# The last b projections of a gated convolution by seven products instead of eight, with their weight sums prepared during attention

## The chip, the cores and the metric

The kernel runs on one core of one Trainium2 chip. The metric is the device time of one execution in microseconds, as the median of several runs. TensorE, the matrix engine, is PE in the profile, and its weight loads are PEld. VectorE is DVE, ScalarE is ACT, GpSimd is POOL, and SyncE, which here only issues transfers, is SP.

## The reference

512 tokens of width 1024 pass through two layers. The first layer's mixer is attention with a forget gate and 16 heads, the second layer's is a short gated convolution; each is followed by an MLP of width 4096 and a gated embedding. What the change touches:

```python
def short_conv(h, w_in, conv_w, w_out):
    proj = h @ w_in
    b_gate, c_gate, u = proj[..., :D], proj[..., D:2 * D], proj[..., 2 * D:]
    z = c_gate * u
    zc = causal depthwise convolution of z with three taps
    return (b_gate * zc) @ w_out
```

All of it is float32.

## The kernel before

Every float32 operand of a matmul is held as two float32r halves, hi and lo, and each product is three matmuls, hi·hi, hi·lo and lo·hi (`mm3`). Each weight tile of 128x512 is loaded by SP into one of 14 `raw` buffers (L148), cast by ACT into its hi half (L299), and subtracted by DVE into its lo half (L300). All other tiles in SBUF come from 70 pages of 128x512 that are used in turn, and results of matmuls go to the eight banks of PSUM.

The 1024 channels of the convolution are eight blocks of 128, called 0 to 7, and they are made in pairs (0,1), (2,3), (4,5) and (6,7). The names of a pair's tiles carry its first channel block. For a pair there are three projections, c, u and b. c and u are made together as a 2 by 2 block product by the Strassen-Winograd scheme: seven products (`PARTS`, 1 to 7) in place of eight, each of 24 matmuls of 256 columns (two output blocks, four blocks of depth, three matmuls each), or 168 matmuls for a pair. It needs sums of tokens, s1 to s4, which DVE makes once (`token_sums`), and sums of weights, t1 to t4, which are made in DRAM. DVE puts each product together with the others as soon as it is there (`COMBINE`, L913), out of the bank into pages. `end` then multiplies c by u (L925), `finish` convolves (ACT L836, DVE L839 twice), multiplies by b (L843) and splits the result into yh and yl (ACT L299, DVE L300). b itself is made directly, by `times_b`: for a pair 2 channel blocks x 8 blocks of depth x 3 matmuls, 48 of 512 columns.

`CONV_ORDER` says in which order products, b and `end` of the pairs are written. Behind it follows `mixer_out`, which multiplies the eight y by the output weights: eight blocks (t, n) of 128 tokens by 512 columns, each the sum over k = 0 to 7 of y of channel block k (24 matmuls of 512 columns), named co0_0 and so on (n and t).

A scheduler with its own model of time sets the order within each engine from the order in which the code is written; each engine then works its list off strictly in that order.

The weight sums are made by DRAM-to-DRAM transfers that POOL issues (`sum_weights`): for each of t1 to t4 and each of the four pairs a copy of 512 KB (L211), and later an accumulating transfer of 512 KB on top of it (L213), 32 in all. They are called one at a time, behind POOL's work in the output of attention, in the MLP of the first layer and in its embedding.

In attention, SP loads for every head the bias rows, four broadcast loads (`bias`, L596) of 64 to 256 KB into pr, prr and prl. POOL masks each (L597). DVE adds the scores to it (L616), ACT exponentiates it, POOL scales it (L622), and PE transposes it (L629).

Of the kernel before, what the change touches and what calls it, by code (L numbers as in the profile page):

```python
# [15 lines left out]
P = 128  # L16
D = 1024
S = 512
# [6 lines left out]
NEG = -1e30  # L25
PUT_OFF = 46000
LAG = 2
AHEAD = 2
STACK = 6
PAGES = 70  # L30
# [59 lines left out]
def trunk(ctx: ExitStack, tc, g4T, x, xT, pT, g, g0T, wv, wqk, bf, wo, wcs, wcb, cw, wco, wup, wdn, wpp, wpg, out):  # L90
# [104 lines left out]
        return ready[key]  # L195

    behind, ahead = {}, {}
    sums_w = {n: dram.tile([4, P, 2 * S], F32, tag=f"ws{n}", name=f"ws{n}") for n in SUMS_W}

    sum_steps = [(name, kind, i) for name, kind in SUM_STEPS for i in range(4)]  # L200

    def sum_weights():

        if not sum_steps:
            return
        of = lambda n, i: sums_w[n][i] if n in sums_w else wcs[QUARTERS.index(n), i]
        name, kind, i = sum_steps.pop(0)
        a, b = SUMS_W[name]
        with tc.issue_after(behind["add"].ins):
            if kind == "copy":  # L210
                nc.gpsimd.dma_start(sums_w[name][i], of(a, i))  # L211
            else:
# [15 lines left out]
    for l in range(2):  # L228
        if l == 0:
            for c, (_, width) in enumerate(V_CHUNKS):  # L230
                for k in range(KT * width // 512 if width < 272 else KT):
                    plan(("v", c, k), wv[c][k])
            for i in range(KT):
                for j in range(4):
                    plan(("qk", i, j), wqk[i, j])
            plan_embed(0)
            for k in range(KT):
                for n in range(2):
                    plan(("o", n, k), wo[n, k])
        else:  # L240
            for i0, i in CONV_ORDER:
                if i == "embed":
                    plan_embed(1)
                elif i == "bL" or i == "b":
                    for j in range(4):
                        plan(("b", i0, j), wcb[i0 // 2, j])
                elif i in PARTS:
                    n = PARTS[i][1]
                    src = sums_w[n] if n in sums_w else wcs[QUARTERS.index(n)]
                    for s in range(2):  # L250
                        plan(("sq", i0, s, n), src[i0 // 2][:, s * S : (s + 1) * S])
            for n in range(2):
                for k in range(KT):
# [182 lines left out]
    def soon(t, n):  # L436

        return FEW if n else SOON

    def mixer_out(kind, lhs, xs, gB, then, opened):  # L440


        mgs, sums = {}, {}
        for t, n in BLOCKS:
            if (t, n) == (2, 0):
                prepare(where[kind, 1, KT - 1] + 1 + SOON)
            at = (t, n) in opened
            ps = opened.pop((t, n)) if at else bank(f"{kind}{n}_{t}")
            for k in range(KT - 1 if at else 0, KT):
                mm3(ps, lhs(k, t), wide(kind, n, k, soon=soon(t, n)), k == 0, k == KT - 1)  # L450
            sums[t, n] = squares(ps, f"{kind}s{n}_{t}")
            mgs[t, n] = gained(ps, gB, n, f"{kind}m{n}_{t}")
            if (t, 1 - n) in mgs:
                residual(t, *([d.pop((t, i)) for i in range(2)] for d in (mgs, sums)), xs[t],
                         f"{kind}r")
                if kind == "o":
                    sum_weights()
                then(t)
                if kind == "o":
                    sum_weights()  # L460

    def embed(l, soon):

# [11 lines left out]
    def attention(hT, first_xT, g0_col, first_x, by_hand):  # L475
# [108 lines left out]
        def bias(h):  # L584


            i, e = h // 2, h % 2
            if e == 0:
                both[i] = page(f"pr{i}")
            long, rest = page(f"prl{h}"), page(f"prr{h}")  # L590
            probs[h] = [
                rest[:, 384:512], both[i][:, 256 * e : 256 * e + 256], rest[:, :384], long[:, :S],
            ]
            for b, pr in enumerate(probs[h]):
                n = (b + 1) * P
                nc.sync.dma_start(pr, neg_c[b, h : h + 1, :n].partition_broadcast(P))  # L596
                nc.gpsimd.affine_select(  # L597
                    out=pr[:, b * P : n], in_=pr[:, b * P : n], compare_op=ALU.is_ge,
                    fill=NEG, base=0, pattern=[[-1, P]], channel_multiplier=1,
                )  # L600
# [215 lines left out]
        return oT[0], banks_o  # L816

    def conv(hT, plain):
        taps = consts.tile([P, KT, 3], F32, tag="taps", name="taps")
        nc.sync.dma_start(taps, cw)  # L820
        ys = []

        def times_b(i0, lo, hi):

# [6 lines left out]
                        hT.at(lambda h: h[:, k, lo:hi]), k == 0, k == KT - 1,  # L831
                    )

        def finish(i, z, y, b):
# [8 lines left out]
            nc.vector.tensor_tensor(out=a[:, :S], in0=b, in1=a[:, :S], op=ALU.mult)  # L843
            split(y.hi[:, :S], y.lo[:, :S], a[:, :S])

        half = S // 2
# [41 lines left out]
        def product(i0, i):  # L888
# [17 lines left out]
            for item in list(rest):  # L906
                out, u, v, sign = item
                if u in have and v in have:
# [6 lines left out]
                        op=ALU.add if sign > 0 else ALU.subtract,  # L915
                    )

        def end(i0):

            have = got.pop(i0)  # L920
            for e in range(2):
                i, z = i0 + e, have[f"c1{e + 1}"]
                for h, at in enumerate((L, R)):
                    m = have[f"c{h + 1}{e + 1}"]
                    nc.vector.tensor_tensor(out=z[:, at], in0=m[:, L], in1=m[:, R], op=ALU.mult)  # L925
                y = Pair(page(f"yh{i}", F32R), page(f"yl{i}", F32R))
                finish(i, z, y, banks_b.pop((i0, e)))
                ys.append(y)

        need(0, 1)  # L930
        for i0, i in CONV_ORDER:
# [315 lines left out]
def layout(x, p, norm_g, w_attn_in, b_forget, w_attn_out, w_conv_in, conv_w, w_conv_out,  # L1247
# [24 lines left out]
    got["wo"] = tiles(np.asarray(w_attn_out)[0], 1, S)  # L1272
    b, c, u = (np.asarray(w_conv_in)[0].reshape(D, 3, KT // 2, 2, P)[:, s] for s in range(3))
    got["wcb"] = tiles(b.reshape(D, D), 2, 256)
    cu = np.stack([c, u]).reshape(2, 2, 4, P, 4, 2, P)
    got["wcs"] = cu.transpose(1, 5, 4, 3, 0, 2, 6)[[0, 0, 1, 1], [0, 1, 0, 1]].reshape(4, 4, P, 2 * S)
# [26 lines left out]
```

## Time and profile before

| what | value |
|---|---|
| median of three runs | 1215.29 us (1214.1 to 1215.66) |
| the profiled execution's own time | 1215.53 us |
| its span, first to last instruction | 1213.8 us |
| PE, DVE, ACT, POOL busy | 99%, 75%, 57%, 55% |
| mean granted clock of PE | 0.999 |

The stretches of the span, in microseconds from its start: attention up to about 225, its output up to about 257, MLP and embedding of the first layer up to 644, the convolution up to 776, its output up to 821, MLP and embedding of the second layer to the end. In the page a busy PE is one whose matmuls overlap: each is shown with a duration longer than its distance from the next, so PE's pace is read from start to start, or from the count in a window.

### The profile page before, as it was taken

The numbers are of one execution on the slowest core, as the hardware profiler recorded it, in microseconds if no ns is written. First come the engines' busy times: TensorE is split into PE (matmuls) and PEld (weight loads), VectorE is DVE, ScalarE is ACT, GpSimd is POOL, SyncE is SP. The second block draws the span as 40 slices with busy tenths as digits, with TensorE's granted clock in tenths as the row PEclk, the third lists the DMA queues.
The fourth block names the chain that finished last, engine by engine and source line by source line (L and its number), as shares of the span: only waits on it lengthen the run. The fifth ranks groups of instructions, "written<-read, shape, count | busy, mean of one in ns | idle before, by whom it ended". The sixth has DMA issues, their size and how long they took to land.

```text
span 1213.8 us, 18739 instructions
## 1 busy us (share of the span) xinstructions
PE 1203.1 (99%) x6176; PEld 1028.0 (85%) x6176; DVE 910.2 (75%) x1389; ACT 697.8 (57%) x1435; POOL 662.3 (55%) x691
## 2 busy tenths in 40 slices
PE   9999999999999999999999999999999999999997
PEld 8888888898888888888889999889888888888886
DVE  5668888575698779869867888665767886679963
ACT  7567888557634654465666555235755445535652
POOL 3057677167977798876221000017769777777420
PEclk9999999999999999999999999999999999999999
DMA  9564442673565566528357445732322442244501
GB/s 308 189 183 128 134 126 65 220 245 94 123 172 140 148 164 173 151 72 264 122 153 212 144 153 172 245 129 81 119 72 88 139 132 80 67 139 130 182 19 52
DMA packets 95377, 173.91 MB, mean 143 GB/s; under 512 B 11248, under 2 KB 18464, under 8 KB 95024
## 3 DMA queue, kind: packets, MB, share of 16 engines
q1 hardware_dynamic: 90272, 155.67, 40.1%
q0 software_dynamic: 4864, 16.78, 6.5%
q8 instruction: 49, 0.80, 0.3%
q14 instruction: 48, 0.39, 0.1%
q10 hardware_dynamic: 144, 0.26, 0.1%
HBM read 164.20 MB, written 25.25 MB: 156 GB/s over the span
## 4 chain that ended last, share of the span: by engine, by line
PE 96%; ACT 2%; DVE 1%; issue 1%; DVEq 0%; POOLq 0%; POOL 0%; ACTq 0%
PE up L293 10%; PE up L292 10%; PE up L291 10%; PE dn L293 9%; PE dn L291 8%; PE dn L292 8%; PE pg L293 2%; PE pg L291 2%; PE pg L292 2%; PE sq L293 2%; PE sq L292 2%; PE sq L291 2%; PE qk L291 2%; PE qk L292 2%; PE qk L293 2%; PE sc L610 1%
## 5 line engine op out<-in xcount | busy, mean ns | idle before, releaser
L300 DVE TENSOR_TENSOR wl<-raw,wh 128x512 fp32r<-128x512 f32 (+1 forms) x400 | 375.0, 980 | 41.7 <-ACT wh L299 37.6
L299 ACT CAST wh<-raw 128x512 fp32r<-128x512 f32 (+1 forms) x400 | 218.3, 619 | 12.4 <-DMA raw<-in_wv 3.7
L292 PE MATMUL up<-hTl,wh 128*128 128x512 f32 (+1 forms) x576 | 209.9, 366 | 0.0
L293 PE MATMUL up<-hTh,wl 128*128 128x512 f32 (+1 forms) x576 | 208.9, 365 | 0.0
L291 PE MATMUL up<-hTh,wh 128*128 128x512 f32 (+1 forms) x576 | 208.7, 366 | 0.0
L300 POOL TENSOR_TENSOR wl<-T,wh 128x512 fp32r<-128x512 f32 x112 | 157.2, 1434 | 25.4 <-ACT wh L299 24.1
L970 ACT ACTIVATE r<-up 128x512 f32<-128x512 f32 (+1 forms) x72 | 39.4, 548 | 197.3 <-PE up L293 197.3
L1018 DVE TENSOR_TENSOR acc<-dn,acc 128x512 f32<-128x512 f32 x168 | 107.8, 678 | 31.1 <-PE dn L293 31.0
L292 PEld LDWEIGHTS up<-hTl,wh 128*128 128x128 f32 x576 | 108.6, 189 | 17.5
L293 PEld LDWEIGHTS up<-hTh,wl 128*128 128x128 f32 x576 | 108.7, 189 | 17.4
L291 PEld LDWEIGHTS up<-hTh,wh 128*128 128x128 f32 x576 | 108.0, 189 | 17.6
L161 POOL TENSOR_TENSOR T<-raw,raw 128x512 f32<-128x512 f32 x56 | 85.8, 1544 | 59.7 <-DMA raw<-in_wdn 28.2
L161 POOL TENSOR_TENSOR T<-raw,T 128x512 f32<-128x512 f32 x56 | 89.0, 1589 | 2.2
L321 POOL TENSOR_SCALAR cor_r_v<-cos,cos 128x1 f32<-128x1 f32 x4 | 1.2, 302 | 155.5 <-ACT junk L337 155.5
L299 ACT CAST wh<-T 128x512 fp32r<-128x512 f32 x112 | 61.5, 617 | 10.4 <-POOL T L161 10.4
L300 DVE TENSOR_TENSOR A12l<-q,A12h 128x512 fp32r<-128x512 f32 x28 | 30.1, 1074 | 42.8 <-ACT A12h L299 42.8
L300 DVE TENSOR_TENSOR A11l<-q,A11h 128x256 fp32r<-128x256 f32 x28 | 26.1, 933 | 35.9 <-ACT A11h L299 35.9
L1025 POOL TENSOR_TENSOR acc<-acc,acc 128x512 f32<-128x512 f32 x28 | 47.1, 1714 | 10.0 <-DVE acc L1018 10.0
L299 ACT CAST S1h<-s 128x512 fp32r<-128x512 f32 x28 | 17.4, 621 | 60.8 <-POOL s L985 60.8
L293 PE MATMUL pg<-wh,hTl 128*128 128x512 f32 (+1 forms) x136 | 51.8, 381 | 0.0
L291 PE MATMUL pg<-wh,hTh 128*128 128x512 f32 (+1 forms) x136 | 51.6, 379 | 0.0
L292 PE MATMUL pg<-wl,hTh 128*128 128x512 f32 (+1 forms) x136 | 51.4, 378 | 0.0
(327 smaller groups left out, 3302.2 us busy)
## 6 DMA issues: line engine op xcount, KB each, us to landing
raw<-in_wup SPq DMA_DIRECT2D x128, 256.0 KB, 2.9
raw<-in_wdn SPq DMA_DIRECT2D x128, 256.0 KB, 2.8
wst<-in_wcs POOLq DMA_DIRECT2D x24, 512.0 KB, 6.7
raw<-in_wqk SPq DMA_DIRECT2D x32, 256.0 KB, 4.8
raw<-in_wpg SPq DMA_DIRECT2D x32, 256.0 KB, 3.2
raw<-wst SPq DMA_DIRECT2D x32, 256.0 KB, 3.6
raw<-in_wcs SPq DMA_DIRECT2D x24, 256.0 KB, 4.0
g<-in_g SPq DMA_DIRECT2D x18, 256.0 KB, 5.4
```

Of the source, the lines that this page charges most:

```text
L161: nc.gpsimd.tensor_tensor(out=B[name, p], in0=B[a, p], in1=B[b, p], op=ALU.subtract)
L291: nc.tensor.matmul(ps, a.hi, b.hi, start=start, stop=False)
L292: nc.tensor.matmul(ps, a.hi, b.lo, start=False, stop=False)
L293: nc.tensor.matmul(ps, a.lo, b.hi, start=False, stop=stop)
L299: nc.scalar.copy(hi, src)
L300: eng.tensor_tensor(out=lo, in0=src, in1=hi.bitcast(F32), op=ALU.subtract)
L321: nc.gpsimd.tensor_scalar(out=v, in0=parts[0], scalar1=parts[1], scalar2=EPS, op0=ALU.add, op1=ALU.add)
L610: nc.tensor.matmul(ps[:, :nm], at[:, b * P : n], to[:, :nm], start=s == 0, stop=s == 1)
L970: nc.scalar.activation(r[:, :n], ps[:, :n], AF.Relu)
L1018: nc.vector.tensor_tensor(out=a, in0=banks[s], in1=a, op=ALU.add)
L1025: nc.gpsimd.tensor_tensor(out=a, in0=a, in1=acc[i, s][:, :S], op=ALU.add)
```

## The change

- `UNITS` adds a fifth unit, "b", beside the four pairs. Its two column halves are b of pair (4,5) and of pair (6,7): b of the last four channel blocks is now made as one block product by the same seven products, and `times_b` is left for pairs (0,1) and (2,3) alone. Its weight sums are made with the others, so there are 20 copies and 20 accumulating transfers in place of 16 and 16.
- `CONV_ORDER` writes the "b" unit behind pair 6: the first two products of each next unit stand ahead of `end` of the one before, and its last product is 2.
- `finish` now ends with the convolution; `weigh` multiplies by b and splits. For channel blocks 4 to 7 it is called in `end("b")`, once all of b is there, in two halves of 256 columns each.
- `mixer_out` for the convolution takes k in the order 0, 1, 2, 3, 4, 6, 5, 7, and writes k = 0 to 3 of the blocks (0,0) and (1,0) first.
- The 20 copies of weight sums are issued by SP during attention, two behind each `bias(h)` from head 2 on (`copy_sums`), until they run out at head 11. POOL issues the 20 accumulating transfers alone, one for each 128 tokens of attention's output and the rest in the first MLP.

```diff
+CO_ORDER = (0, 1, 2, 3, 4, 6, 5, 7)
+CO_FIRST = 4
...
-SUMS_W = {"t1": ("b11", "b12"), "t3": ("b12", "b22"), "t2": ("t1", "b22"), "t4": ("t2", "b21")}
-SUM_STEPS = (
-    ("t1", "copy"), ("t3", "copy"), ("t1", "add"), ("t3", "add"), ("t2", "copy"), ("t2", "add"),
-    ("t4", "copy"), ("t4", "add"),
-)
+SUMS_W = {"t1": ("b11", "b12"), "t3": ("b12", "b22"), "t2": ("b22", "t1"), "t4": ("b21", "t2")}
+UNITS = (0, 2, 4, 6, "b")
...
-    + [(i0, i) for i0 in (4, 6) for i in (1, 6, 7, 5, 2, 4, 3, "b", "end")]
+    + [(4, i) for i in (1, 6, 7, 5, 2, 4, 3)] + [(6, 1), (6, 6), (4, "end")]
+    + [(6, i) for i in (7, 5, 2, 4, 3)] + [("b", 1), ("b", 6), (6, "end")]
+    + [("b", i) for i in (7, 5, 3, 4, 2, "end")]
...
+    def copy_sums():
+
+        if sum_copies:
+            n, u = sum_copies.pop(0)
+            with tc.issue_after(behind["bias"].ins):
+                nc.sync.dma_start(of(n, u), of(SUMS_W[n][0], u))
 
     def sum_weights():
 
-        if not sum_steps:
-            return
...
+        if sum_steps:
+            n, u = sum_steps.pop(0)
+            with tc.issue_after(behind["add"].ins):
                 nc.gpsimd.dma_start(
-                    sums_w[name][i], of(b, i), accum_op=ALU.add, max_dma_last_dim=2048
+                    of(n, u), of(SUMS_W[n][1], u), accum_op=ALU.add, max_dma_last_dim=2048
                 )
...
+        if kind == "co":
+            for t, n in BLOCKS[:2]:
+                ps = bank(f"{kind}{n}_{t}")
+                for k in CO_ORDER[:CO_FIRST]:
+                    mm3(ps, lhs(k, t), wide(kind, n, k, soon=SOON), k == 0, False)
+                opened[t, n] = ps, CO_ORDER[:CO_FIRST]
...
                 if c == 8 * (h // 2) - SCORED - (7 if h % 2 == 0 else 4):
                     bias(h)
+                    copy_sums()
+                    copy_sums()
...
+            if i0 == "b":
+                b = got.pop(i0)
+                for e in range(2):
+                    for i1 in (4, 6):
+                        y = Pair(page(f"yh{i1 + e}", F32R), page(f"yl{i1 + e}", F32R))
+                        weigh(halfway.pop(i1 + e), y, [
+                            (at, b[f"c{h + 1}{e + 1}"][:, R if i1 == 6 else L])
+                            for h, at in enumerate((L, R))
+                        ])
+                        ys[i1 + e] = y
+                return
```

How the instructions move, at the three places that the prediction speaks of. First PE at the passage from the convolution to its output, where b7 is b of channel block 7, and co0_0 the first output block. Before:

```order
L292 MATMUL b7_9467<-hTl_90,wh337_9323 128x512
L293 MATMUL b7_9467<-hTh_89,wl337_9324 128x512
L291 MATMUL co0_0_9574<-wh338_9343,yh0_8507 128x512
L292 MATMUL co0_0_9574<-wl338_9344,yh0_8507 128x512
L293 MATMUL co0_0_9574<-wh338_9343,yl0_8508 128x512
L291 MATMUL co0_0_9574<-wh339_9361,yh1_8518 128x512
```

Now, where sq2_b is product 2 of the new unit and its last:

```order
L297 MATMUL sq2_b_9587<-hTl_90,wh343_9426 128x256
L298 MATMUL sq2_b_9587<-hTh_89,wl343_9427 128x256
L296 MATMUL co0_0_9709<-wh344_9432,yh0_8519 128x512
L297 MATMUL co0_0_9709<-wl344_9433,yh0_8519 128x512
L298 MATMUL co0_0_9709<-wh344_9432,yl0_8520 128x512
```

The 96 matmuls of 512 columns on b4 to b7 are gone from PE's list, and 168 of 256 columns, sq1_b to sq2_b, stand in one piece ahead of the output (6037 rows of matmuls and transposes before, 6109 now).

Second, the first use of the late y. On PE, in the output stage, now (co1_2 is the block of the second column half and the third 128 tokens):

```order
L296 MATMUL co1_2_9881<-wh355_9643,yh3_8819 128x512
L297 MATMUL co1_2_9881<-wl355_9644,yh3_8819 128x512
L296 MATMUL co0_0_9709<-wh348_9550,yh4_9661 128x512
L297 MATMUL co0_0_9709<-wl348_9551,yh4_9661 128x512
L296 MATMUL co0_1_9722<-wh348_9550,yh4_9661 128x512
L298 MATMUL co0_0_9709<-wh348_9550,yl4_9662 128x512
```

The scheduler put not 24 but 60 matmuls of k = 0 to 3, on all six of the first output blocks, between the last sq2_b and the first that reads yh4; yl4 is read by the 64th and yl7 by the 73rd from the first co0_0. On DVE the work between the last product and these y now stands so (cp_b holds the last combination, za4 to za7 the convolved blocks, wl the lo halves of output weights):

```order
L934 TENSOR_TENSOR cp_b_9379<-cp_b_9379,sq2_b_9587 128x512
L305 TENSOR_TENSOR wl356_9650<-raw314_9651,wh356_9649 128x512
L864 TENSOR_TENSOR za5_9181<-U_b_9418,za5_9181 128x256
L864 TENSOR_TENSOR za7_9464<-U_b_9418,za7_9464 128x256
L305 TENSOR_TENSOR wl357_9656<-raw315_9657,wh357_9655 128x512
L864 TENSOR_TENSOR za4_9175<-V_b_9493,za4_9175 128x256
L864 TENSOR_TENSOR za6_9458<-V_b_9493,za6_9458 128x256
L864 TENSOR_TENSOR za4_9175<-cp_b_9379,za4_9175 128x256
L864 TENSOR_TENSOR za6_9458<-cp_b_9379,za6_9458 128x256
L305 TENSOR_TENSOR yl4_9662<-za4_9175,yh4_9661 128x512
L305 TENSOR_TENSOR yl6_9668<-za6_9458,yh6_9667 128x512
```

with yl5 and yl7 behind them. Before, yl4 and yl5 stood ahead of pair 6's products on DVE, and only yl6 and yl7 came this late.

Third, SP in attention, at the bias loads of heads 2 and 3. Before:

```order
L596 DMA prl2_1009<-neg_c_187 128x512
L596 DMA pr1_1008<-neg_c_187 128x256
L596 DMA prr3_1092<-neg_c_187 128x128
L596 DMA prr3_1092<-neg_c_187 128x384
L596 DMA prl3_1091<-neg_c_187 128x512
L148 DMA raw50_2009<-in_wqk 128x512
```

Now:

```order
L609 DMA prl2_1009<-neg_c_187 128x512
L212 DMA wst1_85<-in_wcs 16x8192 x2
L609 DMA pr1_1008<-neg_c_187 128x256
L609 DMA prr3_1094<-neg_c_187 128x128
L609 DMA prr3_1094<-neg_c_187 128x384
L609 DMA prl3_1093<-neg_c_187 128x512
L212 DMA wst1_85<-in_wcs 16x8192 x2
L150 DMA raw50_2025<-in_wqk 128x512
```

Two copies of 512 KB stand between the loads of the even head and those of the odd one, and two more ahead of the next weight loads; so it goes for heads 2 to 11.

More of the change, by code (lines that the diff above doesn't have):

```diff
@@ L197, in trunk @@
     behind, ahead = {}, {}
-    sums_w = {n: dram.tile([4, P, 2 * S], F32, tag=f"ws{n}", name=f"ws{n}") for n in SUMS_W}
-    sum_steps = [(name, kind, i) for name, kind in SUM_STEPS for i in range(4)]
-    def sum_weights():
-        if not sum_steps:
-            return
[L206 to L212, printed above, removed]
+    sums_w = {
+        n: dram.tile([len(UNITS), P, 2 * S], F32, tag=f"ws{n}", name=f"ws{n}") for n in SUMS_W
+    }
+    of = lambda n, u: (sums_w[n] if n in sums_w else wcs[QUARTERS.index(n)])[UNITS.index(u)]
+    sum_copies = [(n, u) for n in ("t1", "t3", "t2", "t4") for u in UNITS]
+    sum_steps = list(sum_copies)
+    def copy_sums():
[3 more added lines that the diff above has]
+                nc.sync.dma_start(of(n, u), of(SUMS_W[n][0], u))
+    def sum_weights():
+        if sum_steps:
+            n, u = sum_steps.pop(0)
+            with tc.issue_after(behind["add"].ins):
                 nc.gpsimd.dma_start(
-                    sums_w[name][i], of(b, i), accum_op=ALU.add, max_dma_last_dim=2048
+                    of(n, u), of(SUMS_W[n][1], u), accum_op=ALU.add, max_dma_last_dim=2048
                 )
@@ L248, in trunk @@
                     n = PARTS[i][1]
-                    src = sums_w[n] if n in sums_w else wcs[QUARTERS.index(n)]
                     for s in range(2):
-                        plan(("sq", i0, s, n), src[i0 // 2][:, s * S : (s + 1) * S])
+                        plan(("sq", i0, s, n), of(n, i0)[:, s * S : (s + 1) * S])
             for n in range(2):
-                for k in range(KT):
+                for k in CO_ORDER:
                     plan(("co", n, k), wco[n, k])
@@ L447, in mixer_out @@
             at = (t, n) in opened
-            ps = opened.pop((t, n)) if at else bank(f"{kind}{n}_{t}")
-            for k in range(KT - 1 if at else 0, KT):
-                mm3(ps, lhs(k, t), wide(kind, n, k, soon=soon(t, n)), k == 0, k == KT - 1)
+            ps, done = opened.pop((t, n)) if at else (bank(f"{kind}{n}_{t}"), ())
+            todo = [k for k in (CO_ORDER if kind == "co" else range(KT)) if k not in done]
+            for k in todo:
+                mm3(
+                    ps, lhs(k, t), wide(kind, n, k, soon=soon(t, n)),
+                    not done and k == todo[0], k == todo[-1],
+                )
             sums[t, n] = squares(ps, f"{kind}s{n}_{t}")
@@ L595, in bias @@
                 n = (b + 1) * P
-                nc.sync.dma_start(pr, neg_c[b, h : h + 1, :n].partition_broadcast(P))
+                behind["bias"] = nc.sync.dma_start(
+                    pr, neg_c[b, h : h + 1, :n].partition_broadcast(P)
+                )
                 nc.gpsimd.affine_select(
@@ L813, in attention @@
                     bias(h)
+                    copy_sums()
+                    copy_sums()
         for _ in main:
             pass
-        return oT[0], banks_o
+        return oT[0], {at: (ps, range(KT - 1)) for at, ps in banks_o.items()}
     def conv(hT, plain):
@@ L842, in finish, with weigh @@
                 )
-            nc.vector.tensor_tensor(out=a[:, :S], in0=b, in1=a[:, :S], op=ALU.mult)
+            return a
+        def weigh(a, y, b):
+            for at, m in b:
+                nc.vector.tensor_tensor(out=a[:, at], in0=m, in1=a[:, at], op=ALU.mult)
             split(y.hi[:, :S], y.lo[:, :S], a[:, :S])
```

19 lines of the change are left out of this document (11 added, 8 removed).

## Prediction

> **What bounds the kernel now.** I read the page first, then PE's busy time by stage, then the convolution stretch by stretch. The page's head, and the head of its chain of waits:
>
> ```profile
> span 1213.8 us, 18739 instructions
> PE 1203.1 (99%) x6176; PEld 1028.0 (85%) x6176; DVE 910.2 (75%) x1389; ACT 697.8 (57%) x1435; POOL 662.3 (55%) x691
> PE 96%; ACT 2%; DVE 1%; issue 1%; DVEq 0%; POOLq 0%; POOL 0%; ACTq 0%
> ```
>
> PE bounds it nearly alone, so a matmul saved is time saved if nothing else comes to the front. PE's idle time by stage (attention; its output, MLP and embedding; convolution with output; the second MLP), each row being stretch, length, and busy time of PE, PEld, DVE, ACT, POOL, then granted clock, DMA share, GB/s:
>
> ```profile
> 60.00:220.00 160.00, 158.44 (x834) 133.42 (x833) 131.44 (x357) 126.68 (x300) 105.52 (x174) 1.00 0.44 131
> 220.00:644.00 424.00, 423.29 (x1999) 354.32 (x1998) 325.10 (x389) 239.65 (x477) 283.70 (x262) 1.00 0.56 160
> 644.00:821.00 177.00, 177.00 (x1160) 162.82 (x1159) 133.44 (x226) 84.02 (x173) 8.54 (x17) 1.00 0.54 175
> 821.00:1206.00 385.00, 385.00 (x1833) 323.77 (x1832) 279.97 (x335) 208.56 (x406) 253.90 (x213) 1.00 0.32 100
> ```
>
> Only attention leaves PE idle for longer: 160 - 158.44 = 1.56 us, and 0.71 in the stage behind it. There is 2.27 us to be won by removing waits; everything else must come from less work. The clock is full, 1.00.
>
> **The matmuls: -1.67.** The convolution's four stretches that the change rewrites are products of pair 4, b4 and b5, products of pair 6, b6 and b7; the fifth is six blocks of the output:
>
> ```profile
> 713.96:734.11 20.15, 20.15 (x169) 20.14 (x168) 16.46 (x28) 10.88 (x20) 0.00 (x0) 1.00 0.47 157
> 734.11:745.02 10.91, 10.91 (x50) 9.02 (x49) 10.87 (x20) 1.87 (x3) 0.00 (x0) 1.00 0.88 297
> 745.02:765.17 20.15, 20.15 (x169) 20.14 (x168) 14.39 (x24) 12.12 (x22) 0.00 (x0) 1.00 0.41 130
> 765.17:776.08 10.91, 10.91 (x50) 9.02 (x49) 10.09 (x18) 1.97 (x3) 0.00 (x0) 1.00 0.94 300
> 776.08:808.73 32.65, 32.65 (x146) 26.99 (x145) 11.96 (x19) 8.49 (x21) 2.09 (x6) 1.00 0.46 160
> ```
>
> 168 narrow products take 20.15 us, 119.9 ns each; 48 of b take 10.91, 227.3 ns each; 144 of the output 32.65, 226.7 ns. (The counts in the rows hold one or two that reach in from the neighbours.) Out go 2 x 10.91 = 21.82 us, in come 168 narrow ones, 20.15: a gain of 1.67 us. One product in eight is gone, but a half-width matmul costs more than half, so 12.5% becomes 7.7%.
>
> The Trainium skill ("TensorE: Matmul & The Clock Gate", Wait — 56ns, not 53.3ns?) has warm matmuls follow each other at N / 2.4 GHz + about 2.5 ns: 215.8 ns for 512 columns and 109.2 for 256. By it the gain would be, as an estimate, 96 x 215.8 - 168 x 109.2 = 2.37 us. The rows above stand 11 ns over it at both widths, and the sum goes by the rows.
>
> **Does DVE keep up?** Durations of its work and of ACT's casts in this stage (the last two figures before the bar's end are total and mean ns):
>
> ```profile
> L300 DVE TENSOR_TENSOR wl<-raw,wh 128x512 fp32r<-128x512 f32 x78 | 49.7, 683 | 11.9 <-ACT wh L299 11.9
> L843 DVE TENSOR_TENSOR za<-b,za 128x512 f32<-128x512 f32 x8 | 5.5, 692 | 0.7
> L913 DVE TENSOR_TENSOR cp<-cp,sq 128x512 f32<-128x512 f32 x6 | 4.1, 682 | 2.8 <-PE sq L293 2.8
> L925 DVE TENSOR_TENSOR cp<-cp 128x256 f32<-128x256 f32 x4 | 1.7, 416 | 0.0
> L299 ACT CAST wh<-raw 128x512 fp32r<-128x512 f32 x79 | 43.0, 619 | 8.5 <-DMA raw<-in_wco 3.0 <-DMA raw<-in_wcs 2.9 <-DVE xb L416 1.9
> ```
>
> Eight b tiles of weights become fourteen: 6 x 0.683 = 4.1 us of DVE and 6 x 0.619 = 3.7 of ACT. Seven combinations are new: 7 x 0.682 = 4.8. Four multiplications by b (0.692) become eight of half width (0.416): +0.6. DVE gains 9.5 us of work over its 16.46 + 10.87 + 14.39 + 10.09 = 51.8 in the four stretches: 61.3 us in a stretch that is now 62.12 - 1.67 = 60.45. DVE is full there, so the last y come later. ACT has 26.8 + 3.7 and stays half idle. When is the last y late? The end of the y on DVE, and PE's first transposes of the stage behind with the DVE work that they read:
>
> ```profile
> 778.32 0.69 DVE L300 TENSOR_TENSOR yl<-za,yh 128x512 fp32r<-128x512 f32 x1 [0.69 <-ACT yh L299]
> 787.77 0.69 DVE L300 TENSOR_TENSOR wl<-raw,wh 128x512 fp32r<-128x512 f32 x1 [8.76 <-ACT wh L299]
> 807.44 0.69 DVE L409 TENSOR_TENSOR n_h<-xb,g 128x512 f32<-128x512 f32 x1
> 808.73 1.03 PE L354 MATMUL n_p<-ident,n_h 128*128 128x128 f32 x8
> ```
>
> Before, yl7 ends at 779.0, and 8.76 us of idle DVE follow. With all 9.5 us on top it ends at 788.5, with none of it at 777.3; laying DVE's rows one behind the other with the durations above and waiting for each product gives about 783. PE now begins the output at 776.08 - 1.67 = 774.41; it first reads yh4 behind 60 matmuls, 774.41 + 60 x 0.2267 = 788.0, and yl7 as the 73rd matmul, at 790.7. So the output matmuls with k = 0 to 3 hide the whole tail, by 2.2 us in the worst case and some 7 us in mine; 0. If that cover were gone (24 matmuls alone, 5.4 us), PE would wait 1 to 2 us, in the worst case 6.
>
> What is late next: co0_0 ends 4 to 5 us later than before (behind 73 matmuls, not 45), and with it the chain of norms that ends in n_h. PE reads it at 808.73 + 0.4, 1 us behind its end at 808.1. The last block that this chain waits for on ACT, co1_2, ends after 121 matmuls of the stage as before after 120, so the chain moves forward with PE; the margin stays between 0 and 1 us, and I give it nothing, with 1 us as the other bound. PSUM: no product waits for a bank, since each bank is read within some 5 us and the next product is 2.9 us long, with eight banks.
>
> **The copies on SP: +0.2.** POOL in the first heads' probabilities and the transposes that read them; SP's bias loads with their landing; waits of POOL's masks and of PE (total, times, longest); the DMA queue of the sums; and attention's output, where the copies ran before:
>
> ```profile
> 84.22 0.29 POOL L597 TENSOR_SCALAR_AFFINE_SELECT prr<-prr 128x128 f32<-128x128 f32 x1
> 85.94 0.29 POOL L597 TENSOR_SCALAR_AFFINE_SELECT prl<-prl 128x128 f32<-128x128 f32 x1
> 87.44 3.10 POOL L622 TENSOR_SCALAR prl<-prl,rs 128x512 f32<-128x512 f32 x2
> ...
> 89.74 0.27 PE L629 MATMUL pT<-ident,prl 128*128 128x128 f32 x1
> ...
> 72.44 3.11 SPq L596 DMA_DIRECT2D prr<-neg_c  x2
> 75.64 0.38 SPq L596 DMA_DIRECT2D prl<-neg_c  x1
> DMA to landing us min/median/max: 6.3/7.0/8.2
> ...
> POOL prr L597 <- DMA prr<-neg_c: 39.3, 6, 27.7
> PE ps_o L651 <- ACT ph L299: 0.8, 2, 0.5
> PE ps_o L652 <- DVE pl L300: 0.4, 1, 0.4
> ...
> q0 software_dynamic: 4864, 16.78, 6.5%
> 234.00:265.00 31.00, 31.00 (x181) 27.32 (x180) 24.47 (x39) 17.05 (x43) 15.17 (x28) 1.00 0.99 354
> ```
>
> No copy on SP is in the trace, so its price is bounded. From below by the rate of the last row: 2 x 0.524 MB / 354 GB/s = 3.0 us of all engines for a pair. From above by the queue: 6.5% of 1213.8 us over 32 transfers of 512 KB is 2.5 us each, 4.9 for a pair. I take 3.5, nearer the rate, since half of the 32 are accumulating and do more. A pair stands ahead of head 3's bias loads, which land by 74.5 + 8.2 = 82.7 and 75.64 + 6.3 = 81.9; POOL asks for them at 84.22 and 85.94, 1.5 to 4 us later. Queued behind that mask on POOL are the scalings (L622) of head 0, whose first prl ends half way through the pair, at 89.0, and PE's transpose reads it at 89.74: 0.75 us to spare. So a pair delays PE here by 0 (3.5 within the spare) up to 4.9 - 1.5 - 0.75 = 2.65 us. In the new order head 3's mask of pr stands behind two scalings on POOL and no longer ahead of them, which gives it 3 us more; I take 0.2. For later heads PE reads what POOL scales many microseconds after, and the weight loads of attention run ahead by up to 14 buffers, so a few microseconds on SP's queue reach nobody.
>
> POOL loses 16 copy issues and gains 4 accumulating ones; 8 of the 16 stood in attention's output, where PE idles next to nothing, the rest in MLP and embedding, where it does not wait for POOL: 0. The loss of 8 x 0.5 MB from the full DMA of 234 to 265 frees nobody that PE waits for: 0.
>
> **Sum:** -1.67 + 0.2 = -1.5. The profiled execution took 1215.53 us for a span of 1213.8, so 1214.0; it stood 0.24 over the median of the runs, which makes 1213.8 as a median. About 0.2%, 2.4 us, is what a measurement can tell from no change.
>
> **Rivals.**
> - *The copies reach PE.* They pass through the queue on which bias and weights come, and a head's last load is not issued before loads eight places ahead have landed. If head 3's loads come a whole pair, 4.9 us, after POOL asks, POOL stands still, the first probabilities are late, and PE loses 4.9 - 0.75 = 4.15: -1.67 + 4.15 = +2.5, 1217.8. It decides from 0.75 us of delay on POOL on. For: POOL is the third engine of this stage, and masks already wait for loads, 11.6 us in five waits beside the first of 27.7. Against: 1.5 to 4 us of spare. The Trainium skill ("DMA: Bandwidth & Descriptors", Queues, rings and completion order) says that each DMA engine serves its queue rows in turn, packet by packet; by it POOL's queue let the loads of SP slip in between, and on SP's own they must stand behind, which speaks for this rival. No row here shows copies on SP. Chance 0.1.
> - *Waits disappear too.* Heads and output of attention are reordered a little, and half of the 2.27 us of PE's idle time goes: -1.67 - 1.1 = -2.8, 1212.5. For: POOL has fewer instructions where PE waits. Against: the waits that the trace names for PE are on ACT and DVE, whose lists stay. Chance 0.15.
> - *The y come too late.* If ACT's 3.7 us add to DVE's 9.5 instead of lying beside them, yl7 ends at 792.2, 1.5 us after PE asks, and the transposes behind lose their margin too: -1.67 + 1.5 + 0.2 = 0, 1215.3. Chance 0.08.
> - *The seven products don't save what they say*, since narrow matmuls run at PEld's limit (20.14 of 20.15 us) and any disturbance of weight loads shows: gain 0.5, 1214.8. Chance 0.05.
>
> **How the numbers follow.** The forecast has 0.6, with its own range of 1213.0 to 1215.0; the rest, 0.02, is a loss that I don't see. The range for 8 in 10 reaches from the bottom of the second rival, 1212.0, to above the case of a PE wait of 2.65 us in attention, 1213.8 - 0.2 + 2.65 = 1216.2: 1212.0 to 1216.4. Faster by over 0.2% means under 1212.9: most of the second rival and the edge of the forecast, 0.2. Slower by over 0.2% means over 1217.7: the first rival's worse half and what I don't see, 0.1. Within: 0.7.
>
> **What would show it.** Right: the four stretches become three of 20.15 us with PE at 119.9 ns, the output begins 1.67 us earlier, DVE busy for nearly the whole of 714 to 783, yl7 before 788; PE's idle time from 60 to 220 within 0.5 us of 1.56. Wrong: a wait of PE for pT or ps_o at 89 to 110, masks on POOL waiting for bias loads of odd heads by more than 1.5 us, a wait of co for yh or yl, or of n_p for n_h.

## The result and the profile after

The change makes the kernel slower by 0.9%: 1226.44 us as a median (1224.92 to 1227.98) against 1215.29 for the kernel before, a ratio of 1.0093 with a 95% interval of 1.0079 to 1.0107. The profiled executions stand 10.5 us apart in their spans. Here and in the experiments, the few executions that took 40% longer or more than the others of the same kernel are left out. The head of the page after, and the head of its chain of waits:

```profile
span 1224.3 us, 18924 instructions
PE 1205.6 (98%) x6248; PEld 1033.6 (84%) x6248; DVE 909.7 (74%) x1406; ACT 700.8 (57%) x1442; POOL 659.6 (54%) x679
PE 91%; DMA 5%; ACT 1%; issue 1%; DVE 1%; SPq 1%; POOL 1%; POOLq 0%; DVEq 0%
```

The chain was 96% PE and now has 5% of DMA in it: somewhere PE follows a transfer. The stretches say where. Columns as in the prediction: attention, then one of its slices and its three stretches at half clock, then the products of pairs 4 and 6, those of unit b, and six blocks of the output.

```profile
60.00:220.00 160.00, 151.15 (x771) 127.11 (x770) 120.01 (x339) 118.91 (x281) 103.97 (x167) 0.97 0.59 182
140.00:160.00 20.00, 18.06 (x93) 15.36 (x91) 13.58 (x41) 13.29 (x34) 13.39 (x22) 0.91 0.83 242
94.31:97.73 3.42, 3.42 (x11) 2.65 (x11) 3.23 (x9) 2.43 (x7) 1.47 (x4) 0.50 0.59 198
111.38:114.79 3.41, 3.41 (x12) 2.82 (x11) 0.63 (x2) 1.18 (x4) 2.41 (x3) 0.50 0.46 154
152.34:155.75 3.41, 3.41 (x12) 2.92 (x13) 0.10 (x2) 0.46 (x1) 3.41 (x4) 0.50 0.93 234
725.95:766.26 40.31, 40.31 (x337) 40.31 (x336) 34.37 (x59) 16.77 (x31) 0.00 (x0) 1.00 0.57 185
766.26:786.42 20.16, 20.16 (x170) 20.16 (x169) 18.95 (x34) 11.18 (x21) 0.00 (x0) 1.00 0.72 216
786.42:819.07 32.65, 32.65 (x146) 27.00 (x145) 16.99 (x32) 10.19 (x24) 2.16 (x4) 1.00 0.63 215
```

The convolution did what was forecast: 40.31 + 20.16 = 60.47 us from the first product of pair 4 to the output, where it was 62.12, so 1.65 us less. Attention lost much more. PE is idle for 160 - 151.15 = 8.85 us of it, 7.3 more than before, and for 10.24 us it runs at half the clock, which costs 5.1 more. Together 7.3 + 5.1 - 1.65 = 10.8, against 10.5 in the spans.

What PE waits for in attention, the list of waits of the kernel after (total, times, longest):

```profile
PE ps_o L666 <- POOL ph L651: 5.4, 3, 3.0
PE pT L644 <- POOL prl L637: 2.7, 1, 2.7
```

The timeline of POOL and PE at the first two of them; "[2.68 <-POOL prl L637]" is the idle time ahead of an instruction and what ended it:

```profile
89.94 0.29 POOL L612 TENSOR_SCALAR_AFFINE_SELECT prl<-prl 128x128 f32<-128x128 f32 x1 [2.00 <-DMA prl<-neg_c]
90.22 1.24 POOL L637 TENSOR_SCALAR prr<-prr,rs 128x384 f32<-128x384 f32 x1
91.44 3.10 POOL L637 TENSOR_SCALAR prl<-prl,rs 128x512 f32<-128x512 f32 x2
93.06 0.33 PE L644 MATMUL pT<-ident,prl 128*128 128x128 f32 x1 [2.68 <-POOL prl L637]
109.54 0.29 POOL L612 TENSOR_SCALAR_AFFINE_SELECT prl<-prl 128x128 f32<-128x128 f32 x1 [0.87 <-DMA prl<-neg_c]
109.77 0.21 POOL L651 MEMSET ph<- 128x128 f32 x1
110.03 0.39 PE L666 MATMUL ps_o<-ph,v 128*128 128x256 f32 x1 [3.00 <-POOL ph L651]
```

It is the chain that the first rival describes. POOL stands at the mask of head 3's prl until its load lands; the scalings of head 0 are queued behind that mask, that of prl begins 4.0 us later than before (91.44, not 87.44), and PE's transpose waits for it. At 109.5 it happens again with head 5, and there a memset of ph is queued behind the mask, which PE reads at once.

The timeline of SP around head 3's loads in the kernel after:

```profile
72.39 2.01 SPq L212 DMA_DIRECT2D wst<-in_wcs  x2
74.44 1.63 SPq L609 DMA_DIRECT2D pr<-neg_c  x1
76.17 1.69 SPq L609 DMA_DIRECT2D prr<-neg_c  x2
77.96 0.53 SPq L609 DMA_DIRECT2D prl<-neg_c  x1
```

How long the last of these loads, issued at 77.96, took to land, by the view of its line:

```profile
DMA to landing us min/median/max: 11.9/11.9/11.9
```

And the same for the four copies around it, by the view of theirs:

```profile
DMA to landing us min/median/max: 9.2/10.9/12.6
```

Before, that load was issued at 75.64 and landed 6.3 us later, at 82.0. Now it is issued 2.3 us later, since SP first issues two copies, which takes it 2.0 us, and it flies 5.6 us longer: it lands at 89.9, 7.9 us late, where the prediction had counted with 3.5 for the pair and 4.9 at most.

It is not one load alone. In the change the last loads of heads 3, 5, 7, 9 and 11 fly 11.4 to 12.2 us, and those of heads 13 and 15, for which no copies are left, 6.2 and 6.5; before, those of heads 3 to 15 fly 6.0 to 8.0. Head 11's, and then head 13's, by the view of their line:

```profile
DMA to landing us min/median/max: 12.0/12.0/12.0
DMA to landing us min/median/max: 6.2/6.2/6.2
```

### The profile page after: what moved, and what is told of

Read it like the earlier page. It is cut to its first block, busy times and chain, and to the rows that moved or that the text cites. A ratio compares the mean times of both kernels' runs of the same rounds, so it can differ in the third digit from the quotient of the medians.

```text
span 1224.3 us, 18924 instructions
## 1 busy us (share of the span) xinstructions
PE 1205.6 (98%) x6248; PEld 1033.6 (84%) x6248; DVE 909.7 (74%) x1406; ACT 700.8 (57%) x1442; POOL 659.6 (54%) x679
## 4 chain that ended last, share of the span: by engine, by line
PE 91%; DMA 5%; ACT 1%; issue 1%; DVE 1%; SPq 1%; POOL 1%; POOLq 0%; DVEq 0%
PE up L296 10%; PE up L298 10%; PE up L297 10%; PE dn L298 8%; PE dn L297 8%; PE dn L296 8%; PE pg L298 2%; PE pg L296 2%; PE pg L297 2%; PE sq L298 2%; PE sq L297 2%; PE sq L296 2%; DMA prl<-neg_c 2%; PE qk L297 1%; PE qk L296 1%; PE o L297 1%
## 5 line engine op out<-in xcount | busy, mean ns | idle before, releaser
L304 ACT CAST wh<-raw 128x512 fp32r<-128x512 f32 (+1 forms) x406 | 221.1, 618 | 8.6 <-DMA raw<-in_wv 4.8
L163 POOL TENSOR_TENSOR T<-raw,T 128x512 f32<-128x512 f32 x56 | 89.9, 1605 | 2.2
L296 PE MATMUL qk<-hTh,wh 128*128 128x512 f32 x128 | 52.3, 408 | 0.0
L298 PE MATMUL qk<-hTh,wl 128*128 128x512 f32 x128 | 51.6, 403 | 0.0
```

Source lines behind the costliest of these rows:

```text
L163: nc.gpsimd.tensor_tensor(out=B[name, p], in0=B[a, p], in1=B[b, p], op=ALU.subtract)
L296: nc.tensor.matmul(ps, a.hi, b.hi, start=start, stop=False)
L298: nc.tensor.matmul(ps, a.lo, b.hi, start=False, stop=stop)
L304: nc.scalar.copy(hi, src)
```

## The experiments

### Which part of the change loses

*The convolution alone.* The 20 copies go back to POOL's queue, to the places where 16 stood before, with a few places more in the output of attention and the first MLP.

```diff
-            with tc.issue_after(behind["bias"].ins):
-                nc.sync.dma_start(of(n, u), of(SUMS_W[n][0], u))
...
+                if kind == "copy":
+                    nc.gpsimd.dma_start(of(n, u), of(SUMS_W[n][0], u))
```

> The change without its copies on SyncE: 20 copies go back to GpSimd's queue, in attention's output, the first MLP and the embedding, as 16 did before; the convolution is that of the change. Theory A (the loads of attention stand behind the copies on SyncE's queue) and theory B (the bytes of the copies slow every load in flight, on whichever queue) both say: the loss is gone and the convolution's gain stands alone, 1215.3 - 1.67 = 1213.6 us (1213.0 to 1214.4), PE idle for about 1.6 us of the 160 us from 60 to 220, granted clock 1.00 there. Theory C (the loss, or a part of it, sits in the convolution or in what is made late there) says 1217 or more.

*The copies alone.* The kernel before, its convolution untouched, with 16 copies issued by SP in attention.

```diff
+                nc.sync.dma_start(of(n, i), of(SUMS_W[n][0], i))
...
+                    copy_sums()
+                    copy_sums()
```

> The kernel before, with its 16 copies moved to SyncE's queue in attention as in the change (two behind the bias loads of each head from 2 to 9); the convolution is the old one. Theories A and B: the loss alone, without the gain. The trace of the change shows 8.9 - 1.6 = 7.3 us more of PE's idle time in attention and about 4.4 us of halved clock behind the waits; with 16 of 20 copies some four fifths of 11.7, so 1225 us (1222 to 1229). Theory C: 1215.5, as before.

Measured: the convolution alone took 1216.02 us (ratio 1.0008, 0.9999 to 1.0018), the copies alone 1225.38 (1.0089, 1.0072 to 1.0105). Attention's row with the convolution alone:

```profile
60.00:220.00 160.00, 158.62 (x836) 133.76 (x835) 131.80 (x358) 126.87 (x301) 102.68 (x173) 1.00 0.45 129
```

The same row with the copies alone:

```profile
60.00:220.00 160.00, 151.23 (x781) 126.94 (x780) 123.26 (x343) 120.23 (x285) 104.32 (x168) 0.98 0.56 172
```

PE's longest waits there, with the copies alone:

```profile
PE ps_o L654 <- POOL ph L639: 5.5, 2, 4.9
PE pT L632 <- POOL prl L625: 2.3, 1, 2.3
```

The copies in attention make the loss, with the old convolution as with the new one: without them attention's row is as it was. But 1216.02 lies in neither of the ranges for the convolution alone, 1213.0 to 1214.4 and, by theory C, 1217 or more; C goes out only with the kernels below that have the new convolution and copies behind odd heads, 1214.08 and 1214.38. So the convolution alone did not show its gain as a time: 1213.6 was expected. Its profiled span is 1213.5, 0.3 under the one before instead of 1.65. In all of its executions 2.0 us of the time lie outside the span and in all of the kernel before 1.7 to 1.8; where these 0.3 us come from is not known. And among its waits of PE from 220 to 660 is one that the kernel before has not, in the first MLP, where POOL now issues more transfers:

```profile
PE dn L296 <- DVE S1l L303: 1.2, 1, 1.2
```

That POOL's added issues delay what PE waits for there is argued from this one row, not shown.

### Queue, place, pieces or bytes

*Another queue.* ACT issues the same copies on its own queue, each behind an exponential at about the same time.

```diff
-            with tc.issue_after(behind["bias"].ins):
-                nc.sync.dma_start(of(n, u), of(SUMS_W[n][0], u))
+            with tc.issue_after(behind["exp"].ins):
+                nc.scalar.dma_start(of(n, u), of(SUMS_W[n][0], u))
...
```

> The change, with the same 20 copies of the same bytes issued at about the same times by ACT on its own DMA queue, each behind an exponential of the scores, not by SyncE. Theory A: the bias loads no longer stand behind copies; they land nearly as before (head 3's last at about 82 us, not 89.9), PE's idle time from 60 to 220 is back within 1.5 us of 1.6, and the time is 1213.6 to 1216. Theory B: the engines are as full as in the change, the loads as late, 1222 to 1228.

Measured: 1226.51 us (1.0096, 1.0081 to 1.0111), so theory A is out. The timeline: two copies on ACT's queue, SP's issue of head 3's prl, with no copy ahead of it on SP's own queue, and POOL's mask of it:

```profile
76.10 0.60 ACTq L212 DMA_DIRECT2D wst<-in_wcs  x1
76.75 0.60 ACTq L212 DMA_DIRECT2D wst<-in_wcs  x1
76.98 0.32 SPq L609 DMA_DIRECT2D prl<-neg_c  x1
90.41 0.29 POOL L612 TENSOR_SCALAR_AFFINE_SELECT prl<-prl 128x128 f32<-128x128 f32 x1 [3.50 <-DMA prl<-neg_c]
```

That load's line, issue to landing:

```profile
DMA to landing us min/median/max: 13.4/13.4/13.4
```

It took 13.4 us, longer than behind the copies on SP's queue. So a load is held up also when no copy stands ahead of it on its queue. The Trainium skill ("DMA: Bandwidth & Descriptors", Issuing engines are not separate DMA queues) says that, whichever engine issues, the transfers run on the same 16 DMA engines and interleave. This run agrees with it: the load is as late with the copies on the other queue.

*Another place.* The copies stay on SP, but only behind the loads of odd heads, three at each.

```diff
-                    copy_sums()
-                    copy_sums()
+                    for _ in range(3 if h % 2 else 0):
+                        copy_sums()
```

> The change, with the copies still on SyncE, but only behind the bias loads of odd heads, three at each (heads 3 to 15). The next bias loads on the queue come some 13 us later, so three copies of 1.2 to 2.5 us are through by then. Theory A: no head's loads stand behind copies that were issued right ahead of them; PE waits at most 2 us more than before, 1213.6 to 1216. Theory B: the same bytes in attention, 1221 to 1228.

Measured: 1214.08 us, a ratio of 0.9988 (0.9979 to 0.9998). Attention's row:

```profile
60.00:220.00 160.00, 158.76 (x837) 133.71 (x835) 130.90 (x358) 127.05 (x301) 107.10 (x172) 1.00 0.63 195
```

SP's timeline with head 3's last load and the three copies behind it:

```profile
75.52 0.51 SPq L609 DMA_DIRECT2D prl<-neg_c  x1
76.07 4.43 SPq L212 DMA_DIRECT2D wst<-in_wcs  x3
```

The flight of that load, by the view of its line:

```profile
DMA to landing us min/median/max: 8.9/8.9/8.9
```

The same 20 copies on the same queue in the same stage, at a DMA share of 0.63, cost nothing here: PE is idle for 1.24 us. So theory B as it was put, the same bytes in attention and the same loss, is out too. But the load of head 3, which stands *ahead* of the copies on the queue, took 8.9 us and not 6.3. The last loads of heads 5 to 15 fly 7.0 to 11.0 us in this run, where they flew 6.0 to 8.0 before. Copies slow what flies beside them, also what was issued before them; but here the loads are late by less than what they have to spare. From this theory D was made (it is the bytes in flight that slow the loads), and theory E as its rival (it is the long pieces of the copies). Four runs tell them apart.

*Smaller pieces.* Each copy in 256 pieces of 2 KB, not 16 of 32 KB.

```diff
-                nc.sync.dma_start(of(n, u), of(SUMS_W[n][0], u))
+                nc.sync.dma_start(of(n, u), of(SUMS_W[n][0], u), max_dma_last_dim=2048)
```

> The change, each copy of 512 KB cut into 256 pieces of 2 KB, as the weight loads are, where it has 16 pieces of 32 KB that hold a DMA engine for 1.22 us each in the change; queue, places and bytes stay. Theory D (bytes: while a copy is in flight, every load in flight with it is slowed, on whichever queue, and PE loses when the odd heads' loads are late by more than their spare of 1.5 to 4 us): head 3's last load still lands 5 us or more later than the 82.0 of before, 1222 to 1228 us. Theory E (pieces: it is the long ones that hold the engines up for the loads' small ones): it lands by 85, PE loses next to nothing, 1213.6 to 1217.

*One copy per head.*

```diff
-                    copy_sums()
-                    copy_sums()
+                    for _ in range(1 if h < H - 1 else 7):
+                        copy_sums()
```

> The change with one copy behind each head's bias loads from 2 to 14 where it has two, and the last seven behind head 15; queue and pieces stay. Theory D: half as much in flight with each load, so head 3's last load is late by some 4 us where the change has 7.9, about its spare; PE loses 0 to 3 us, 1213.6 to 1217. A rival on the dose (any copy ahead of an odd head's loads holds them up, however short): 1221 or more.

*Even heads.* Three copies just ahead of the loads of each odd head.

```diff
-                    copy_sums()
-                    copy_sums()
+                    for _ in range(0 if h % 2 else 3):
+                        copy_sums()
```

> The mirror of the kernel with copies at odd heads: three copies behind the bias loads of each even head from 2 to 14, so just ahead of the loads of an odd head; number, bytes, queue and pieces are the same. Theory D: the odd heads' loads, those with the small spare, fly with three copies; head 3's last load lands at 88 or later and PE waits at most pairs, 1222 to 1234. A rival (the count of places decides: seven clusters of three do little wherever they stand): 1213.6 to 1217.

*Half the size.* Two copies at each place as in the change, each of 64 of the 128 rows; the other rows behind head 15.

```diff
+            rows = slice(64 * half, 64 * half + 64)
...
-                nc.sync.dma_start(of(n, u), of(SUMS_W[n][0], u))
+                nc.sync.dma_start(of(n, u)[rows], of(SUMS_W[n][0], u)[rows])
...
```

> The change with the same number of copies at the same places, two behind each head's bias loads from 2 to 11, but each of only half the rows, 256 KB in 16 pieces of 16 KB; the other halves are copied behind head 15, where no bias loads follow. Theory D (bytes in flight): what one copy per head did, so head 3's last load lands some 4 us late, at about 86, and the time is 1213.6 to 1217.5. A rival (the number of transfers on the queue decides, not their bytes): it lands at 89 or later and the time is 1221 or more.

Measured: small pieces 1229.29 us (1.0122, 1.0102 to 1.0143), one per head 1216.14 (1.0008, 0.9999 to 1.0018), even heads 1224.70 (1.0082, 1.0066 to 1.0098), half the size 1215.47 (1.0000, 0.9990 to 1.0009). Head 3's last load in all kernels, sorted by when it lands (issue and flight in us, from SP's rows and the landing rows; idle is PE's from 60 to 220):

| kernel | issued | flight | lands | late by | PE idle | ratio |
|---|---|---|---|---|---|---|
| before | 75.64 | 6.3 | 82.0 | | 1.56 | 1 |
| odd heads, three | 75.52 | 8.9 | 84.4 | 2.4 | 1.24 | 0.9988 |
| one per head | 76.97 | 8.8 | 85.8 | 3.8 | 2.44 | 1.0008 |
| two of half the size | 78.20 | 7.7 | 85.9 | 3.9 | 2.16 | 1.0000 |
| the change | 77.96 | 11.9 | 89.9 | 7.9 | 8.85 | 1.0093 |
| ACT's queue | 76.98 | 13.4 | 90.4 | 8.4 | 9.61 | 1.0096 |
| even heads, three | 78.47 | 12.2 | 90.7 | 8.7 | 10.92 | 1.0082 |
| small pieces | 78.78 | 12.1 | 90.9 | 8.9 | 11.47 | 1.0122 |

The flight of that load with small pieces:

```profile
DMA to landing us min/median/max: 12.1/12.1/12.1
```

With three copies at even heads:

```profile
DMA to landing us min/median/max: 12.2/12.2/12.2
```

With copies of half the size:

```profile
DMA to landing us min/median/max: 7.7/7.7/7.7
```

PE's waits for POOL in attention with one copy per head:

```profile
PE ps_o L666 <- POOL ph L651: 1.9, 2, 1.4
```

Theory D gave the landings beforehand: half the bytes beside the loads, 4 us late; three copies beside the odd heads' loads, 88 or later. Of the four times, that with small pieces missed its range, 1222 to 1228, by 1.3 us upwards. Up to 3.9 us late little is lost, and the trace of before had 4.0 us between that landing and POOL's mask. (All kernels of the table but the first have the new convolution. Beside the one with copies behind odd heads, 0.9988, one per head loses 0.2%, with 1.9 us of waits, and half the size 0.1%.) From 7.9 on, everything behind the mask is late. Long pieces are not the cause, since short ones do at least as much harm; theory E is out. The half-size run splits the lateness in two: the issue is as late as in the change (78.20, since as many copies stand ahead on SP), while the flight is longer by 1.4 us, not 5.6.

### What the convolution is worth

Two kernels with copies behind odd heads, three at each: the first is the kernel before with its old convolution and 16 copies, the second is the change with the new one. The edit of the second, against the change:

```diff
-                    copy_sums()
-                    copy_sums()
+                    for _ in range(3 if h % 2 else 0):
+                        copy_sums()
```

> The kernel before with its 16 copies on SyncE behind the bias loads of odd heads, three at each (heads 3 to 13); the convolution is the old one. Theory D: copies at this place cost PE nothing, so 1215.1 us (1214.3 to 1215.6), at most some tenths faster than before, because GpSimd issues 16 copies fewer. If the copies themselves were worth something, 1214 or less.

> The change with its 20 copies behind odd heads, a second time beside the same copies with the old convolution. The difference of the two is the convolution's share of the change: by the trace's products -1.67 us, so 1213.4 to 1214.2, and under the kernel before on the same chip. A rival (the seven products save less in the median than in a profile): a difference under 0.7 us.

The old convolution took 1215.33 us (0.9999, 0.9990 to 1.0008), the new one 1214.38 (0.9993, 0.9984 to 1.0002), and the kernel before 1215.31. The spans of the profiled executions are 1213.6 and 1212.1. So the copies at odd heads are free, as expected, and the convolution brings 1.5 us in a profile and 1.0 in the medians. The new one's time lies 0.2 above its range, 1213.4 to 1214.2, and the ten executions of each kernel scatter by 2 us, so that this pair decides neither for the 1.67 of the products nor for the rival's 0.7. In the first run of the new one it was 1.2 under before. The kernel with copies behind odd heads is the fastest of all here, by about 0.1%, at the edge of what can be measured.

## Why the prediction was wrong

The prediction was 1213.8 us, in a range up to 1216.4; the time is 1226.44.

- **The matmuls, -1.67:** right. 1.65 in the trace of the change; in medians about 1.0, and where the rest goes isn't settled.
- **DVE and the last y, 0:** right. After the change the last yl end at 794.7, 8.3 us behind the begin of the output, where the prediction's 783 meant 8.6. PE asks for yh4 at 786.42 + 60 x 0.2267 = 800.0, so the cover holds with 5.3 us to spare, and no wait of co is in the trace. The stretch of six output blocks is 32.65 us as before, so the margin of the norms behind it held too. But DVE was busy for 53.3 of the 60.47 us (34.37 + 18.95), where the prediction had work for 61.3 and called DVE full; the tail came out by laying DVE's rows one behind the other, not by a full DVE.

```profile
792.23 2.50 DVE L305 TENSOR_TENSOR yl<-za,yh 128x512 fp32r<-128x512 f32 x4 [0.43 <-ACT yh L304]
```

- **The copies on SP, +0.2:** this is the step that failed. It cost 7.3 us of idle time and 5.1 of half clock, 12.4 in all (12.2 by the spans, 10.5 + 1.65). It was wrong in five ways:
  - *The price.* A pair was priced by its bytes through the DMA, 3.0 to 4.9 us, as if the loads stood still for that long and then went on as before. In fact the load itself flies longer beside copies, 11.9 us and not 6.3; SP's issue of head 3's four loads takes no longer, 4.1 us from first to last in both kernels. The second pair, behind head 3's own loads, was left out, though it flies beside them as much as the first. The upper bound of 4.9 was none.
  - *The spare.* Its lower end, 1.5 us, joined the flight of one load, 8.2, to the issue of another, 74.5. The load issued at 74.45 flew 6.9 us and landed at 81.4; POOL asked for it at 85.70, so the spare was 4.3 us there and 4.0 for prl. This made the estimate more careful, and it was still far too low.
  - *The row that was there.* The trace of before has loads of bias beside other traffic: behind those of heads 0 and 1 SP issues weight loads of 256 KB from 58.6 on. The last bias load there, issued at 57.52, took this long to land, by the view of its line:

```profile
DMA to landing us min/median/max: 9.6/9.6/9.6
```

  Against 6.3 for the same load of head 3, with no weight load behind it for 6 us, and 6.0 to 8.0 for those of the later odd heads. Read so, traffic beside a load had a price of about 3 us in the trace.
  - *The later heads.* "For later heads PE reads what POOL scales many microseconds after": true of the scalings, but the memsets of ph stand in the same list of POOL, behind the same masks, and PE reads the one at 109.77 within 0.3 us. Three of the four waits are theirs.
  - *The clock.* A PE wait was counted at its length. Three of the waits were followed by 3.41 us at half clock, 1.7 us each on top, by the three rows at 0.50.
- **POOL's issues, 0:** right where they were taken away (the old convolution with copies at odd heads stands at 1215.33 against 1215.31).
- **The first rival** named place, chain and sign. Its cause was wrong: it held the copies' order on SP's queue responsible, with the Trainium skill's rule on queue rows served in turn ("DMA: Bandwidth & Descriptors", Queues, rings and completion order), by which another queue would have let the loads slip in between. On ACT's queue the loads were just as late. And its price, 4.15 us, was for one wait at one place.
- **Waits disappear too:** at most 0.3 us did, with copies at odd heads (1.24 us of idle time, not 1.56).
- **The sum:** 10.8 us by the terms as measured against -1.5. Without the failed step it would be -1.65, and the kernel with copies at odd heads is where the forecast was, 1214.1 and 1214.4 against 1213.8.

What stays open is which part of the memory system the loads and the copies share. The DMA engines were busy for 0.59 of attention in the change and 0.63 with copies at odd heads, so they were not full on average. While head 3's last load flew they were busy for 0.46 of the time before, 0.75 with copies at odd heads, 0.72 in the change and 0.82 with the copies on ACT's queue. Reading and writing weren't tried apart.

## What to carry to other kernels

Price a moved transfer by what it does to the small loads beside it, not by its own bytes over the bandwidth: find a load in the trace that flies beside other traffic and compare it with one that flies alone. Then look for a gap in the list of loads and put it there; the same 20 copies lost 11 us or nothing, depending on whether they made a load later than the 4 us that it had to spare. Changing the queue or cutting the pieces didn't help; fewer bytes at a place did.

## What the runs showed of the hardware

Waits of PE that are shorter than 3.4 us can halve its clock, and need not. In the change the waits of 2.68 and 3.00 us, and a third of 1.94 that ends at 152.32 (the row from 140 to 160 has 18.06 us of PE in 20), were each followed by a stretch of 3.41 us at half clock. In the run with small pieces PE waits 2.88 us from 109.20 on, and the clock stays at 1.00:

```profile
112.08 0.39 PE L666 MATMUL ps_o<-ph,v 128*128 128x256 f32 x1 [2.88 <-POOL ph L651]
```

The traces show what tells the two apart. The three stretches of the change begin at 94.31, 111.38 and 152.34, so 17.07 and 40.96 us apart, which is 5 and 12 times 3.413: the clock changes on a fixed beat, whenever the waits come. These are the beats just ahead of the three stretches, with PE idle for 2.16, 2.07 and 1.94 us:

```profile
90.90:94.31 3.41, 1.25 (x7) 1.22 (x8) 2.01 (x9) 2.42 (x7) 3.41 (x3) 1.00 0.64 228
107.97:111.38 3.41, 1.34 (x6) 1.17 (x7) 1.13 (x7) 0.96 (x4) 2.54 (x5) 1.00 0.85 331
148.93:152.34 3.41, 1.47 (x8) 0.90 (x6) 2.23 (x5) 2.95 (x7) 2.38 (x5) 1.00 0.93 363
```

With small pieces there is one stretch at half clock, up to 99.97, and the third beat behind it ends at 110.21, within the wait of 2.88 us. So the wait is shared out to two beats, 1.01 and 1.87 us, and the clock isn't halved after either:

```profile
93.14:99.97 6.83, 5.88 (x17) 5.01 (x18) 4.27 (x11) 3.82 (x9) 4.05 (x5) 0.50 0.72 198
106.80:110.21 3.41, 2.40 (x11) 1.60 (x9) 2.81 (x7) 3.32 (x6) 3.22 (x7) 1.00 1.00 329
110.21:113.62 3.41, 1.54 (x7) 1.33 (x8) 1.05 (x7) 0.88 (x4) 3.00 (x5) 1.00 0.73 244
113.62:117.03 3.41, 3.41 (x21) 2.89 (x20) 1.31 (x3) 1.45 (x4) 2.82 (x4) 1.00 0.73 116
```

Counted in this way over all twelve traces, every beat at full clock with 1.94 us or more without a matmul is followed by half clock, and none with 1.87 or less is. What a wait costs by the clock thus depends on where it falls in the beat. The half clock lasts two beats, 6.83 us, where PE's wait reaches into the first of them, as it does here by 0.94 us (6.83 - 5.88).

The Trainium skill ("TensorE: Matmul & The Clock Gate", What's actually happening) has the clock halved after at least one idle window of about 3.4 us, by a window that runs freely. The beat of 3.41 us agrees with that. That a whole window must be idle does not agree: 1.94 to 2.16 us of it were enough in the change, and the measurement decides.

SP's own issue of a load is also not a constant: in the kernel before 0.38 us for prl at 75.64, and 3.11 for the two loads of prr ahead of it, without any copy; in the change 1.63 for pr at 74.44.
